# A decoder layer with 32 experts on one core: TensorE branches over an expert's third group of 32 slots where its list has at most 64 tokens

## The chip, the core and the metric

The kernel runs on one core of a Trainium2 chip. The metric is the device time of one execution in microseconds (us), the median of three runs. Engines are named as the profile names them: PE is TensorE (its weight loads apart as PEld), DVE is VectorE, ACT is ScalarE, POOL is GpSimd, and SP is SyncE, which here only issues transfers. A q behind a name is the engine's sequencer.

## What is computed

One decoder layer on 512 tokens of 1024 features, in float32: three kinds of attention, an output projection, a layer norm, and then a mixture of 32 experts of which each token takes four. The change touches the experts only. Cut to them:

```python
logits = xf @ router_w + router_b            # 512 x 32
top_v, top_e = lax.top_k(logits, 4)
gate_w = softmax(top_v)
...
def expert(e, tokens):                       # for each of 32 experts, its own tokens
    h = x[tokens] @ w_gu[e] + b_gu[e]        # 1024 -> 2048
    gate, up = h[:, 0::2], h[:, 1::2]
    gate = minimum(gate, 7); up = clip(up, -7, 7)
    return ((up + 1) * gate * sigmoid(1.702 * gate)) @ w_dn[e] + b_dn[e]   # 1024 -> 1024
...
x = layer_norm(alpha * x + sum over a token's experts of gate_w * expert)
```

512 tokens with four experts each make 2048 places, 64 an expert on average. Counted from the reference's own router on its inputs, the lists of experts 0 to 31 have 53, 68, 76, 65, 61, 70, 53, 58, 66, 59, 76, 79, 83, 69, 44, 60, 72, 70, 64, 45, 63, 66, 95, 43, 40, 73, 75, 73, 76, 44, 66 and 43 tokens. Fourteen have at most 64: experts 0, 4, 6, 7, 9, 14, 15, 18, 19, 20, 23, 24, 29 and 31. None has more than 96.

## The kernel before

The first part of the run is the attention, the router and the lists of tokens. Then `moe` goes through the experts in order. Each expert has room for `NG` = 3 groups of `SL` = 32 slots; a list that is longer than 96 would go through a loop of extra blocks at the end (line 1125 on), which is jumped over with these inputs.

Weights stay in float32 and come through a ring of 18 buffers of 1024 KB (`wring`), in the order in which they are used: per expert eight for gate_up and four for down. `ring(...).get(k)` hands out the next buffer and at once writes the transfer of the tile 18 places on, which SP can issue only when TensorE has finished with the buffer that it takes. All of these transfers stand in one queue, SP's.

For an expert, three indirect transfers on POOL gather its token rows (`gather`), TensorE transposes them (`transposed`, tile `xt`, copied out of PSUM by ACT), `gate_up` makes the bias and eight weight tiles' products for the three groups into PSUM tile `gu`, `act` does the clamped SwiGLU on DVE and ACT (`ga`), TensorE transposes that (`at`), `down` makes the second product into PSUM tile `ya`, ACT scales it by the gates, and three indirect transfers add it to the sum in memory (`accd`). The innermost loop of both products runs over four column quarters, which share the array:

```python
for g in range(NG):
    for c in range(NQ):
        nc.tensor.matmul(ps[SL * c:SL * (c + 1), g, :], lhs(g), w[:, c * 512:(c + 1) * 512], ...)
```

A float32 product is two matmuls on the chip, so the trace has 192 of them for an expert's gate_up (8 tiles, 3 groups, 4 quarters, twice) and 192 for its down. The products are pipelined over experts: TensorE does gate_up of expert e, the transposes of the next expert's rows, then down of expert e - 1, and then the transposes of `ga` of expert e. The routing for two experts at a time (`plan`) lies between.

Of the kernel before, what the change touches and what calls it, by code (L numbers as in the profile page):

```python
# [7 lines left out]
FT = mybir.dt.float32  # L8
I32 = mybir.dt.int32
# [909 lines left out]
def moe(ctx, tc, env):  # L919
# [10 lines left out]
    pst = ctx.enter_context(tc.tile_pool(name="pst", bufs=3, space=PSUM))  # L930
    nring = len(slots)

    def fetch_next(pin=False):
        if state["next"] < len(order):
            fetch(slots[state["next"] % nring], pin)
# [22 lines left out]
            nc.sync.dma_start(accd.rearrange("(s c) d -> s (c d)", c=NQ)[t * P:(t + 1) * P, :], x1all[:, t, :])  # L958

    nbi = rt.tile([P, NE + 1], I32, name="nbi")  # L960

    def count():
        cnt = rt.tile([P, NE], FT, name="cnt")
        cp = pst.tile([P, 512], FT, name="cp", tag="tr")
        for t in range(NT):
            nc.tensor.matmul(cp[:, :NE], routing.on, routing.msk[:, t, :], start=(t == 0), stop=(t == NT - 1))
        nc.vector.tensor_copy(cnt, cp[:, :NE])
        nbf = rt.tile([P, NE + 1], FT, name="nbf")
        nc.vector.tensor_scalar(nbf[:, :NE], cnt, float(CAP), None, op0=OP.is_gt)
        cge = rt.tile([P, NE], FT, name="cge")  # L970
        for b in range(2, -(-S // CAP)):
            nc.vector.tensor_scalar(cge, cnt, float(CAP * b), None, op0=OP.is_gt)
            nc.vector.tensor_add(nbf[:, :NE], nbf[:, :NE], cge)
        nc.vector.tensor_reduce(nbf[:, NE:], nbf[:, :NE], AX.X, OP.max)
        nc.vector.tensor_copy(nbi, nbf)

    bases = [1] + list(range(2, NE, 2))
    ixs, gwt = ({0: [v[:, 0, g:g + 1] for g in range(NG)]} for v in (routing.ix0, routing.gw0))
# [40 lines left out]
    def listed(xt, k, g):  # L1019

        return xt[:, 2 * g + k % 2, SL * (k // 2):SL * (k // 2 + 1)]

    def gate_up(xt, weights, pick):
        ps = psg.tile([P, NG, 512], FT, name="gu", tag="gu")

        def column_tiles(lhs, w, start, stop):
            for g in range(NG):
                for c in range(NQ):
                    nc.tensor.matmul(ps[SL * c:SL * (c + 1), g, :], lhs(g), w[:, c * 512:(c + 1) * 512], start=start,  # L1029
                                     stop=stop)  # L1030

        column_tiles(lambda g: pick.to_broadcast([G, SL]), bpart, True, False)
        for k in range(8):
            w = weights(k).rearrange("p a c -> p (a c)")
            column_tiles(lambda g: listed(xt, k, g), w, False, k == 7)
        return ps

    def act(ps):
# [8 lines left out]
        nc.vector.scalar_tensor_tensor(ga, up, 1.0, ga, op0=OP.add, op1=OP.mult)  # L1047
        return ga.rearrange("p g f -> p (g f)")

    def down(at, weights, ix, gw):  # L1050
        ya = psg.tile([P, NQ, 256], FT, name="ya", tag="ya")
        for k in range(8):
            if k % 2 == 0:
                w = weights(k // 2)
            for g in range(NG):
                for c in range(NQ):

                    nc.tensor.matmul(ya[SL * c:SL * (c + 1), g, :], listed(at, k, g), w[:, k % 2, c * 256:(c + 1) * 256],  # L1058
                                     start=(k == 0 and g % 2 == 0), stop=(k == 7), skip_group_check=True)
        y = mk.tile([P, 768], FT, name="y", tag="y", bufs=1)  # L1060
        sc = []
        for g in range(NG):
            cs = slice(g * 256, (g + 1) * 256)
            nc.scalar.activation(y[:, cs], ya[:, g, :], AF.Copy, scale=gw[g])  # L1064
            sc.append(nc.gpsimd.indirect_dma_start(out=accd, out_offset=bass.IndirectOffsetOnAxis(ap=ix[g], axis=0),  # L1065
                                                   in_=y[:, cs], in_offset=None, bounds_check=NQ * S - 1,
                                                   oob_is_err=False, compute_op=OP.add))
        for a, b in ((0, 1), (0, 2), (1, 2)):
            tc.declare_no_dep(sc[b].ins, sc[a].ins, reason="a token is in an expert's list once")
# [28 lines left out]
    start_sum(start)  # L1098
    count()
    xt = transposed(xgs.pop(1), "xt", 1)  # L1100
    for e in range(1, NE + 1):
        at = transposed(hid, "at", 2)
        if e < NE:
            if e + 2 < NE:
                begin(e + 2)
            ps = gate_up(xt, ring("gu", e), bsel[:, e:e + 1])
            if e + 1 < NE:
                xt = transposed(xgs.pop(e + 1), "xt", 1)
        down(at, ring("dn", e - 1), ixs[e - 1], gwt[e - 1])
        if e < NE:  # L1110
            hid = act(ps)

# [3 lines left out]
    g2, b2 = gb[:, 0], gb[:, 1]  # L1116


    more = ctx.enter_context(tc.tile_pool(name="more", bufs=2))
    w_gate_up, w_down = env["w_gate_up"], env["w_down"]  # L1120
    wm = [slots[-1].tile([P, 2, 1024], FT, name=f"wm{k}", tag="wring") for k in range(4)]
    why = "a count of blocks, at most ceil(S / CAP)"
# [1 line left out]
    some = nc.values_load(nbi[0:1, NE:NE + 1], min_val=0, max_val=nmax, skip_runtime_bounds_check_because=why)  # L1124
    with tc.If(some > 0):  # L1125
        with tc.For_i(0, NE) as e:
            pick = more.tile([G, 1], BF, name="pick", bufs=1)
            nc.vector.tensor_copy(pick, bsel[:, bass.ds(e, 1)])
            col = more.tile([P, NT], FT, name="col", bufs=1)
            cval = more.tile([P, NT, 5], BF, name="cval", bufs=1)  # L1130
            nc.vector.tensor_copy(col[:, None, :], routing.pos[:, bass.ds(e, 1), :])
            nc.vector.tensor_copy(cval[:, None], routing.val[:, bass.ds(e, 1), :, :])
            nb = nc.values_load(nbi[0:1, bass.ds(e, 1)], min_val=0, max_val=nmax,
# [1 line left out]
            with tc.For_i(0, nb):  # L1135
                nc.vector.tensor_scalar(col, col, -float(CAP), None, op0=OP.add)
                ip = pst.tile([P, 512], FT, name="ixp", tag="tr")
                a = mk.tile([P, NT, NG * P], BF, name="places", tag="places")
                routing.places(a, col)
                routing.listed(ip, 0, lambda t: a[:, t], cval)  # L1140
                v = more.tile([P, 1, NG, 5], FT, name="vm", bufs=1)
                nc.vector.tensor_copy(v, ip[:, :5 * NG].rearrange("p (e g v) -> p e g v", g=NG, v=5))
                ix = more.tile([P, 1, NG], I32, name="ixm", bufs=1)
                gw = more.tile([P, 1, NG], FT, name="gwm", bufs=1)
                routing.rows(msm, v, 1, ix)
                routing.gates(msm, v, 1, gw)
                ixg = [ix[:, 0, g:g + 1] for g in range(NG)]

                def stream(src, view):
                    def get(k):  # L1150
                        t = wm[k % 4]
                        nc.sync.dma_start(t, view(src, k))
                        return t
                    return get

                def gu_view(w, k):
# [66 lines left out]
```

## Time and profile before

| what | value |
|---|---|
| median of 3 runs | 1503.4 us (1502.09 to 1503.58) |
| the profiled execution, its own time | 1510.97 us |
| its span | 1509.2 us |
| mean granted clock of TensorE | 0.974 |
| TensorE busy | 1434.4 us, 95% of the span |
| share of 16 DMA engines taken by the hardware queue | 74.8% |

The profile is of one execution, some 7.6 us longer than the median of the timed runs. Busy time of an engine is the union of its instructions' spans; matmuls overlap each other, so the mean length of one is far more than what one costs. [...]

### The profile page before, as it was taken

The page shows a single profiled execution, that of the slowest core. Times are in us where ns is not written, and L with a number is a line of the kernel's source. Part 1 is how long each engine was busy: PE and PEld are TensorE (multiplying, and loading weights), DVE is VectorE, ACT ScalarE, POOL GpSimd, SP SyncE. Part 2 cuts the span into 40 slices and gives each one's busy share as a digit, 9 for nine tenths or more (in the row PEclk, how much of TensorE's full clock was granted, in tenths as well). Part 3 has the DMA queues.
Part 4 walks back from the last instruction along what each step waited for, and adds up shares of the span by engine and source line. Part 5 has one row for each costly group of instructions (what it writes and reads, how often), then busy time and mean ns, then how long its engine had stood idle before and what let it go on. Part 6 is the DMA issues. An engine that isn't in the chain of part 4 may idle for free. (4 is left out here: it accounts for less than half of the span.)

```text
span 1509.2 us, 35054 instructions
## 1 busy us (share of the span) xinstructions
PE 1434.4 (95%) x15619; PEld 725.7 (48%) x15620; DVE 413.2 (27%) x887; ACT 294.8 (20%) x683; POOL 391.7 (26%) x331
## 2 busy tenths in 40 slices
PE   8999999985999999999999999999999999999991
PEld 7777667981343444444444444444444434444450
DVE  3585565564221212112020212022020212110004
ACT  5474366530000100100000010011000001000100
POOL 5432323344021212132221212132321212121124
PEclk9999999996899999999999999999999999999996
DMA  8210216547899999999999999999999999999913
GB/s 223 66 32 2 61 40 223 184 156 272 329 358 400 373 394 378 391 380 377 384 377 393 383 400 373 388 381 381 387 382 379 383 397 375 384 375 371 369 17 117
DMA packets 126257, 454.12 MB, mean 301 GB/s; under 512 B 21416, under 2 KB 53642, under 8 KB 93334
## 3 DMA queue, kind: packets, MB, share of 16 engines
q1 hardware_dynamic: 107526, 435.00, 74.8%
q0 software_dynamic: 18432, 16.84, 5.6%
q8 instruction: 124, 2.03, 0.5%
q14 instruction: 31, 0.25, 0.0%
q10 hardware_dynamic: 144, 0.00, 0.0%
HBM read 441.26 MB, written 18.87 MB: 305 GB/s over the span
## 5 line engine op out<-in xcount | busy, mean ns | idle before, releaser
L1029 PE MATMUL gu<-wring,xt 128*32 128x512 f32 x6144 | 684.7, 595 | 1.4 <-issue 0.4
L1029 PEld LDWEIGHTS gu<-wring,xt 128*32 128x32 f32 x6144 | 211.6, 110 | 449.4 <-issue 419.3
L1065 POOL DMA_INDIRECT accd<-y,ix x96 | 151.8, 1581 | 847.9 <-ACT y L1064 828.4
L1058 PE MATMUL ya<-wring,at 128*32 128x256 f32 x6144 | 340.9, 380 | 1.4 <-ACT at L1016 1.4
L1058 PEld LDWEIGHTS ya<-wring,at 128*32 128x32 f32 x6144 | 195.8, 110 | 135.2 <-issue 7.2
L1041 DVE TENSOR_SCALAR ga<-gu 128x768 f32<-128x768 f32 x32 | 30.6, 958 | 779.0 <-PE gu L1029 779.0
L1016 ACT COPY xt<-tp 128x512 f32<-128x512 f32 x64 | 27.6, 482 | 679.5 <-PE tp L1015 614.4
L1005 POOL DMA_INDIRECT xg<-x1d,ix x96 | 100.7, 1049 | 32.3 <-issue 27.1
L1064 ACT ACTIVATE y<-ya,gw 128x256 f32<-128x256 f32 x96 | 38.5, 472 | 296.1 <-issue 219.3
L173 POOL TENSOR_TENSOR wl<-raw,wh 128x1024 fp32r<-128x1024 f32 (+2 forms) x28 | 68.1, 2439 | 93.8 <-ACT wh L170 93.8
L880 DVE TENSOR_TENSOR places<-slot,pos 128x1536 bf16<-128x1536 bf16 x31 | 54.2, 1752 | 106.8 <-PE ixp L890 106.8
L244 PE MATMUL pjt<-xh,wh 128*128 128x512 f32 (+1 forms) x136 | 52.8, 388 | 1.0 <-DVE xl L222 1.0
L244 PE MATMUL pjt<-xh,wl 128*128 128x512 f32 (+1 forms) x136 | 52.4, 385 | 0.0
L244 PE MATMUL pjt<-xl,wh 128*128 128x512 f32 (+1 forms) x136 | 52.1, 383 | 0.0
L170 ACT CAST wh<-raw 128x1024 fp32r<-128x1024 f32 (+2 forms) x28 | 29.5, 1054 | 52.9 <-issue 20.9
L1015 PEld LDWEIGHTS tp<-ident,xg 128*128 128x128 f32 x192 | 21.1, 145 | 36.8 <-issue 35.7
L1015 PE MATMUL tp<-ident,xg 128*128 128x128 f32 x192 | 30.9, 293 | 6.6 <-DMA xg<-x1d,ix 6.6
L1045 ACT ACTIVATE sg<-ga 128x768 f32<-128x768 f32 x32 | 27.4, 855 | 44.1 <-DVE ga L1041 43.7
L430 ACT ACTIVATE pr<-pr,nm 128x256 f32<-128x256 f32 (+3 forms) x64 | 33.8, 529 | 7.5 <-DVE nm L429 6.9
L1046 DVE TENSOR_TENSOR ga<-ga,sg 128x768 f32<-128x768 f32 x32 | 30.7, 958 | 12.0 <-ACT sg L1045 11.5
L1047 DVE SCALAR_TENSOR_TENSOR ga<-up,ga 128x768 f32<-128x768 f32 x32 | 30.6, 958 | 1.1
L1015 PE MATMUL tp<-ident,ga 128*128 128x128 f32 x192 | 30.6, 289 | 0.0
(323 smaller groups left out, 1313.0 us busy)
## 6 DMA issues: line engine op xcount, KB each, us to landing
wring<-in_w_gate_up_dram SPq DMA_DIRECT2D x256, 1024.0 KB
wring<-in_w_down_dram SPq DMA_DIRECT2D x128, 1024.0 KB
raw<-in_w_in_dram SPq DMA_DIRECT2D x16, 512.0 KB
raw<-in_w_out_dram SPq DMA_DIRECT2D x8, 512.0 KB
x1all<-in_x_dram SPq DMA_DIRECT2D x4, 512.0 KB
x1d<-x1all SPq DMA_DIRECT2D x4, 512.0 KB
accd<-x1all SPq DMA_DIRECT2D x4, 512.0 KB
x1all<-accd SPq DMA_DIRECT2D x4, 512.0 KB
```

The lines of the kernel that those rows point to most:

```text
L173: eng.tensor_tensor(l[:, :m], raw[:, :m], h[:, :m].bitcast(FT), op=OP.subtract)
L244: nc.tensor.matmul(ps[:, qs], a[:, k, :], b[:, k, qs], start=(k == 0 and n_ == 0), stop=(k == 7 and n_ == 2))
L430: nc.scalar.activation(pr[:, :n], pr[:, :n], AF.Exp, bias=nm, scale=-1.0, accum_out=den)
L880: ins = self.nc.vector.tensor_tensor(a, self.slot[:, None, :].to_broadcast([P, n, NG * P]), pos[:, :, None].to_broadcast([P, n, NG * P]), ...
L1005: nc.gpsimd.indirect_dma_start(out=xg[:, g * 256:(g + 1) * 256], out_offset=None, in_=x1d, in_offset=bass.IndirectOffsetOnAxis(ap=ix[g], a ...
L1015: nc.tensor.transpose(pt[:, u * P:(u + 1) * P], src[:, (a + u) * P:(a + u + 1) * P], ident)
L1029: nc.tensor.matmul(ps[SL * c:SL * (c + 1), g, :], lhs(g), w[:, c * 512:(c + 1) * 512], start=start, stop=stop)
L1041: nc.vector.tensor_scalar(ga, v[:, :, :, 0], 7.0, None, op0=OP.min)
L1046: nc.vector.tensor_mul(ga, ga, sg)
L1058: nc.tensor.matmul(ya[SL * c:SL * (c + 1), g, :], listed(at, k, g), w[:, k % 2, c * 256:(c + 1) * 256], start=(k == 0 and g % 2 == 0), sto ...
L1064: nc.scalar.activation(y[:, cs], ya[:, g, :], AF.Copy, scale=gw[g])
L1065: sc.append(nc.gpsimd.indirect_dma_start(out=accd, out_offset=bass.IndirectOffsetOnAxis(ap=ix[g], axis=0), in_=y[:, cs], in_offset=None, b ...
```

## The change

The products are split by group. Groups 0 and 1 are always made; group 2 stands in a part of its own, behind a branch that only TensorE takes on a flag of the expert (`thr`, 1 where the count is over 64). Gate_up has two such branches an expert, one after each four weight tiles, and down has one, after its four tiles. The flag is read into a register once an expert. Expert 0, which runs ahead of the loop, and the extra blocks have no branch. PSUM tiles `gu` and `ya` are made once instead of once an expert. Everything else, the gathers, transposes, `act`, the scaling and the scatters, still covers three groups. A variable `more` was renamed `extra`, which changes nothing.

```diff
+    gups = psg.tile([P, NG, 512], FT, name="gu")
+    yaps = psg.tile([P, NQ, 256], FT, name="ya")
...
+    thr = rt.tile([P, NE], I32, name="thr")
...
+        nc.vector.tensor_scalar(thr, cnt, float(2 * SL), None, op0=OP.is_gt)
...
+    def third(e):
+
+        return nc.values_load(thr[0:1, e:e + 1], engines=[mybir.EngineType.PE], min_val=0, max_val=1,
+                              skip_runtime_bounds_check_because="the result of a comparison")
+
+    def groups(more, full, part):
+
+        full()
+        if more is None:
+            part()
+        else:
+            with tc.If(more > 0):
+                part()
...
-        column_tiles(lambda g: pick.to_broadcast([G, SL]), bpart, True, False)
-        for k in range(8):
-            w = weights(k).rearrange("p a c -> p (a c)")
-            column_tiles(lambda g: listed(xt, k, g), w, False, k == 7)
+        def rows(w, k, gs):
+            if k == 0:
+                column_tiles(lambda g: pick.to_broadcast([G, SL]), bpart, True, False, gs)
+            column_tiles(lambda g: listed(xt, k, g), w, False, k == 7, gs)
+
+        for k0 in (0, 4):
+            ws = {}
+
+            def full():
+                for k in range(k0, k0 + 4):
+                    ws[k] = weights(k).rearrange("p a c -> p (a c)")
+                    rows(ws[k], k, range(2))
+
+            groups(more, full, lambda: [rows(w, k, range(2, NG)) for k, w in ws.items()])
...
+        ws = []
+
+        def full():
+            for k in range(0, 8, 2):
+                ws.append(weights(k // 2))
+                rows(ws[-1], k, range(2))
+
+        groups(more, full, lambda: [rows(w, 2 * k, range(2, NG)) for k, w in enumerate(ws)])
...
+            more[e] = third(e)
+            ps = gate_up(xt, ring("gu", e), bsel[:, e:e + 1], more[e])
...
+        down(at, ring("dn", e - 1), ixs[e - 1], gwt[e - 1], more.pop(e - 1, None))
```

The order in which the instructions stand shows what this makes of an engine's program. Names like DMAHW3_49 are the semaphores of transfers, and PE_49 is the one that TensorE raises as its matmuls end; a number behind x counts equal rows, one row here being one float32 product. On PE before, the second half of expert 2's gate_up, weight tiles 4 to 7:

```order
L1029 MATMUL gu_4531<-wring_4090,xt_4334 32x512 [waits DMAHW3_49]
L1029 MATMUL gu_4531<-wring_4090,xt_4334 32x512 x11
L1029 MATMUL gu_4531<-wring_4104,xt_4334 32x512 [waits DMAHW4_49]
L1029 MATMUL gu_4531<-wring_4104,xt_4334 32x512 x11
L1029 MATMUL gu_4531<-wring_4222,xt_4334 32x512 [waits DMAHW1_49]
L1029 MATMUL gu_4531<-wring_4222,xt_4334 32x512 x11
L1029 MATMUL gu_4531<-wring_4236,xt_4334 32x512 [waits DMAHW2_49]
L1029 MATMUL gu_4531<-wring_4236,xt_4334 32x512 x11
L1015 MATMUL tp_4657<-ident_62,xg0_3863 128x128 [waits DMASW1_49,Activation_49]
```

The same place on PE in the changed kernel. Here the row behind the compare is where the program goes on for a long list; the last unconditional branch belongs to the other path, which a short list jumps to:

```order
L1048 MATMUL gu_3862<-wring_4215,xt_4341 32x512 [waits DMAHW1_49]
L1048 MATMUL gu_3862<-wring_4215,xt_4341 32x512 x7
L1048 MATMUL gu_3862<-wring_4233,xt_4341 32x512 [waits DMAHW2_49]
L1048 MATMUL gu_3862<-wring_4233,xt_4341 32x512 x7
L1039 COMPARE_AND_BRANCH
L1048 MATMUL gu_3862<-wring_4084,xt_4341 32x512 x4
L1048 MATMUL gu_3862<-wring_4094,xt_4341 32x512 x4
L1048 MATMUL gu_3862<-wring_4215,xt_4341 32x512 x4
L1048 MATMUL gu_3862<-wring_4233,xt_4341 32x512 x4
L1039 UNCONDITIONAL_BRANCH
L1039 UNCONDITIONAL_BRANCH [waits PE_49]
L1020 MATMUL tp_4667<-ident_62,xg0_3866 128x128 [waits DMASW1_49,Activation_49]
```

Each tile's twelve products have become eight ahead of the compare and four behind it, so all four tiles are in use until the part's end. The path for a long list ends in a jump and has no wait; the path for a short list waits for PE_49, raises it for the products that were left out, and goes on.

On SP before, the transfers into the ring behind expert 1's products, with what each waits for:

```order
L85 DMA wring<-in_w_gate_up_dram 128x2048 [waits DMAHW3_49,PE_49]
L85 DMA wring<-in_w_gate_up_dram 128x2048 [waits DMAHW4_49,PE_49]
L85 DMA wring<-in_w_gate_up_dram 128x2048 [waits DMAHW5_49,PE_49]
L85 DMA wring<-in_w_gate_up_dram 128x2048 [waits DMAHW6_49,PE_49]
L85 DMA wring<-in_w_down_dram 128x2x1024 [waits DMAHW7_49,PE_49]
L85 DMA wring<-in_w_down_dram 128x2x1024 [waits DMAHW0_49,PE_49]
L85 DMA wring<-in_w_down_dram 128x2x1024 [waits DMAHW1_49,PE_49]
L85 DMA wring<-in_w_down_dram 128x2x1024 [waits DMAHW2_49,PE_49]
```

And the same transfers on SP in the changed kernel:

```order
L85 DMA wring<-in_w_gate_up_dram 128x2048 [waits DMAHW3_49,PE_49]
L85 DMA wring<-in_w_gate_up_dram 128x2048 [waits DMAHW4_49,PE_49]
L1039 UNCONDITIONAL_BRANCH
L85 DMA wring<-in_w_gate_up_dram 128x2048 [waits DMAHW5_49,PE_49]
L85 DMA wring<-in_w_gate_up_dram 128x2048 [waits DMAHW6_49,PE_49]
L85 DMA wring<-in_w_down_dram 128x2x1024 [waits DMAHW7_49]
L1039 UNCONDITIONAL_BRANCH
L85 DMA wring<-in_w_down_dram 128x2x1024 [waits DMAHW0_49,PE_49]
L85 DMA wring<-in_w_down_dram 128x2x1024 [waits DMAHW1_49,PE_49]
L85 DMA wring<-in_w_down_dram 128x2x1024 [waits DMAHW2_49,PE_49]
L1039 UNCONDITIONAL_BRANCH
```

Their order is the same, but a plain branch of SP's own stands between them wherever TensorE has one, and some transfers have lost their wait for TensorE: their buffer comes free together with that of the transfer ahead.

## Rows read from the trace of the kernel before

**Rows 1.** The page: span, busy us (share) xinstructions, DMA tenths in 40 slices.

```profile
span 1509.2 us, 35054 instructions
PE 1434.4 (95%) x15619; PEld 725.7 (48%) x15620; DVE 413.2 (27%) x887; ACT 294.8 (20%) x683; POOL 391.7 (26%) x331
...
DMA  8210216547899999999999999999999999999913
```

**Rows 2.** Stretches: us, busy PE PEld DVE ACT POOL, granted clock, DMA share, GB/s.

```profile
322.00:326.90 4.90, 2.87 (x28) 2.69 (x26) 4.44 (x12) 0.55 (x2) 2.29 (x2) 1.00 0.26 107
326.90:330.30 3.40, 3.40 (x18) 3.40 (x18) 2.55 (x12) 1.28 (x4) 0.00 (x0) 0.50 0.09 31
376.00:392.00 16.00, 15.75 (x114) 4.75 (x107) 5.79 (x8) 0.84 (x1) 0.00 (x0) 0.99 1.01 419
404.00:408.00 4.00, 4.00 (x44) 1.20 (x40) 0.00 (x0) 0.00 (x0) 0.00 (x0) 1.00 0.84 297
452.00:472.00 20.00, 20.00 (x284) 10.01 (x280) 3.74 (x4) 3.56 (x8) 2.94 (x2) 1.00 1.01 412
500.00:1380.00 880.00, 878.67 (x10712) 369.03 (x10706) 144.48 (x202) 91.01 (x205) 202.99 (x156) 1.00 1.01 383
```

**Rows 3.** Waits from 404 to 1430 us: total, times, longest.

```profile
DVE ga L1041 <- PE gu L1029: 726.9, 30, 30.6
...
PE gu L1029 <- issue: 0.4, 1, 0.4
```

**Rows 4.** The transfer queue's own waits, 404 to 1430 us: total, times, longest.

```profile
SPq L85 <- PE gu L1029: 444.6, 184, 4.9
SPq L85 <- PE ya L1058: 277.1, 115, 3.1
SPq L85 <- PE tp L1015: 84.5, 33, 3.0
```

**Rows 5.** TensorE's timeline, 466 to 546 us: start, length, line, tiles, count.

```profile
468.62 0.83 PE L1029 MATMUL gu<-bpart,bsel 96*32 96x512 bf16 x12
469.28 20.77 PE L1029 MATMUL gu<-wring,xt 128*32 128x512 f32 x192
...
490.79 10.57 PE L1058 MATMUL ya<-wring,at 128*32 128x256 f32 x192
```

**Rows 6.** TensorE's timeline, 396 to 427 us, expert 1's gate_up.

```profile
399.13 22.22 PE L1029 MATMUL gu<-wring,xt 128*32 128x512 f32 x192
```

**Rows 7.** The timeline of all engines, from 1425 us to the end.

```profile
1431.88 20.98 PE L1029 MATMUL gu<-wring,xt 128*32 128x512 f32 x192
...
1465.97 10.57 PE L1058 MATMUL ya<-wring,at 128*32 128x256 f32 x192 [1.37 <-ACT at L1016]
...
1476.66 1.21 ACT L1064 ACTIVATE y<-ya,gw 128x256 f32<-128x256 f32 x3 [10.46 <-PE ya L1058]
```

**Rows 8.** The page, DMA queues: packets, MB, share of 16 engines.

```profile
q0 software_dynamic: 18432, 16.84, 5.6%
q8 instruction: 124, 2.03, 0.5%
```

**Rows 9.** Lines 1124 and 1125: duration ns min/median/max, first and last start.

```profile
L1124 PEldq TENSOR_LOAD <-nbi x1: 484/484/484, 1475.1 to 1475.1; - x1
L1125 PEldq EVENT_SEMAPHORE  x2: 51/51/51, 1479.3 to 1479.5; - x2
L1125 DVEq COMPARE_BRANCH  x1: 72/72/72, 1456.5 to 1456.5; - x1
L1125 PEldq COMPARE_BRANCH  x1: 3602/3602/3602, 1475.7 to 1475.7; - x1
L1125 ACTq COMPARE_BRANCH  x1: 45/45/45, 1477.3 to 1477.3; - x1
```

**Rows 10.** The issue of weight transfers (line 85), 403.3 to 1430 us.

```profile
L85 SPq DMA_DIRECT2D wring<-in_w_gate_up_dram x234: 327/328/341, 403.4 to 1402.9; - x117
L85 SPq DMA_DIRECT2D wring<-in_w_down_dram x124: 367/373/423, 408.5 to 1425.0; - x124
```

More of the change, by code (lines that the diff above doesn't have):

```diff
@@ L1021, in listed, with gate_up, column_tiles @@
         return xt[:, 2 * g + k % 2, SL * (k // 2):SL * (k // 2 + 1)]
[L1023 to L1027, printed above, removed]
+    def third(e):
[8 more added lines that the diff above has]
+                part()
+    def gate_up(xt, weights, pick, more=None):
+        ps = gups
+        def column_tiles(lhs, w, start, stop, gs):
+            for g in gs:
                 for c in range(NQ):
@@ L1048, in act, with down, rows @@
         return ga.rearrange("p g f -> p (g f)")
[L1050 to L1059, printed above, removed]
+    def down(at, weights, ix, gw, more=None):
+        ya = yaps
+        def rows(w, k0, gs):
+            for k in (k0, k0 + 1):
+                for g in gs:
+                    for c in range(NQ):
+                        nc.tensor.matmul(ya[SL * c:SL * (c + 1), g, :], listed(at, k, g),
+                                         w[:, k % 2, c * 256:(c + 1) * 256], start=(k == 0 and g % 2 == 0),
+                                         stop=(k == 7), skip_group_check=True)
+        ws = []
[4 more added lines that the diff above has]
+        groups(more, full, lambda: [rows(w, 2 * k, range(2, NG)) for k, w in enumerate(ws)])
         y = mk.tile([P, 768], FT, name="y", tag="y", bufs=1)
@@ L1100, in moe @@
     xt = transposed(xgs.pop(1), "xt", 1)
+    more = {}
     for e in range(1, NE + 1):
@@ L1105, in moe @@
                 begin(e + 2)
-            ps = gate_up(xt, ring("gu", e), bsel[:, e:e + 1])
+            more[e] = third(e)
+            ps = gate_up(xt, ring("gu", e), bsel[:, e:e + 1], more[e])
             if e + 1 < NE:
                 xt = transposed(xgs.pop(e + 1), "xt", 1)
-        down(at, ring("dn", e - 1), ixs[e - 1], gwt[e - 1])
+        down(at, ring("dn", e - 1), ixs[e - 1], gwt[e - 1], more.pop(e - 1, None))
         if e < NE:
@@ L1116, in moe @@
     g2, b2 = gb[:, 0], gb[:, 1]
-    more = ctx.enter_context(tc.tile_pool(name="more", bufs=2))
+    extra = ctx.enter_context(tc.tile_pool(name="more", bufs=2))
     w_gate_up, w_down = env["w_gate_up"], env["w_down"]
@@ L1126, in moe @@
         with tc.For_i(0, NE) as e:
-            pick = more.tile([G, 1], BF, name="pick", bufs=1)
+            pick = extra.tile([G, 1], BF, name="pick", bufs=1)
             nc.vector.tensor_copy(pick, bsel[:, bass.ds(e, 1)])
-            col = more.tile([P, NT], FT, name="col", bufs=1)
-            cval = more.tile([P, NT, 5], BF, name="cval", bufs=1)
+            col = extra.tile([P, NT], FT, name="col", bufs=1)
+            cval = extra.tile([P, NT, 5], BF, name="cval", bufs=1)
             nc.vector.tensor_copy(col[:, None, :], routing.pos[:, bass.ds(e, 1), :])
@@ L1140, in moe @@
                 routing.listed(ip, 0, lambda t: a[:, t], cval)
-                v = more.tile([P, 1, NG, 5], FT, name="vm", bufs=1)
+                v = extra.tile([P, 1, NG, 5], FT, name="vm", bufs=1)
                 nc.vector.tensor_copy(v, ip[:, :5 * NG].rearrange("p (e g v) -> p e g v", g=NG, v=5))
-                ix = more.tile([P, 1, NG], I32, name="ixm", bufs=1)
-                gw = more.tile([P, 1, NG], FT, name="gwm", bufs=1)
+                ix = extra.tile([P, 1, NG], I32, name="ixm", bufs=1)
+                gw = extra.tile([P, 1, NG], FT, name="gwm", bufs=1)
                 routing.rows(msm, v, 1, ix)
```

## The prediction

> **What bounds the kernel now.** I read the page first, then the stretches, then the waits of the expert stage. The page shows TensorE busy for 95% of the span, and the DMA slices near full from slice 12 on [rows 1]. The share over the span does not say which of the two sets the pace, so I read the expert stage by itself: between 500 and 1380 us TensorE is busy 878.67 of 880 us at full clock, while the DMA share is 1.01 at 383 GB/s [rows 2]. Both look full. The waits decide it: between 404 and 1430 us TensorE waits for a weight tile in no row (its largest matmul wait is 0.4 us, on its own issue) [rows 3], whereas the transfer queue waits for TensorE to free a slot of the ring, 444.6, 277.1 and 84.5 us in three rows [rows 4]. So TensorE sets the pace; the transfers follow slot by slot.
>
> The pace: from the start of gate_up's weights for expert 1, 399.13 us [rows 6], to that for expert 31, 1431.88 us [rows 7], are 30 experts, 34.4 us each.
>
> But the transfers have little room. Weights alone ran at 419 GB/s in 376 to 392 us and at 412 GB/s in 452 to 472 us [rows 2]. An expert has 12 transfers of 1024 KB, 12.58 MB, which at 415 GB/s take 30.3 us. Gathers and scatters (the software queue) take 5.6% of the span [rows 8], 84.5 us or 2.64 us per expert. Together 32.96 us, 2.747 us per transfer slot, against TensorE's 34.4. That is 4% of room.
>
> **The change, part by part.** *What is skipped.* Gate_up's matmuls take 20.77 us, the bias 0.83, the down product 10.57 us per expert [rows 5]. A third of each is 6.92, 0.28 and 3.52, in all 10.72 us. Thirteen of the experts 1 to 31 have at most 64 tokens; expert 0 has too, but it is outside the branch. 13 x 10.72 = 139.4 us of TensorE work.
>
> *Branches that are not skipped*, 18 experts x 3 = 54. The sequencer loads the flag once an expert, compares, and jumps over two instructions at the end of the part. The only register load and compare on TensorE in this trace are those at the end: the load begins at 1475.08 us and takes 484 ns [rows 9], while the last matmuls run to 1465.97 + 10.57 = 1476.54 us [rows 7]. So the sequencer was 1.46 us ahead of the array, and a load plus a compare (45 ns on ACT, 72 on DVE [rows 9]) fit inside. I take 0.1 us each, 5.4 us; bounds 0 and 0.6 us (nothing hidden). The rows on the order show that no wait stands in this path.
>
> *Branches that are skipped*, 13 x 3 = 39. Here a wait is added: the other path raises TensorE's semaphore for the matmuls that were left out, and first waits until all earlier ones have ended. Behind it on TensorE stands the next half or the transposes. ScalarE starts 0.12 us after the last matmul's end (1476.66 against 1476.54) [rows 7]; the semaphore instruction takes 51 ns on TensorE, a near branch 45 to 72 ns [rows 9], and I add 0.2 us, an estimate, for two matmuls (20.77 us / 192 = 0.108 us each) until the array is full again. I take 0.45 us, 17.6 us in all; bounds 0.2 us and TensorE's own compare of 3602 ns [rows 9].
>
> Why I take the near price: that compare jumped over the whole loop of extra blocks, which holds a gate_up and a down product, 192 matmuls and 192 weight loads each by the rows of an expert, 768 instructions. The instruction queue brought 124 packets in 2.03 MB [rows 8], for 31239 TensorE instructions [rows 1], about 252 a packet. The far jump spans three packets; the new ones skip 64 to 128 instructions, half a packet at most. [...]
>
> *TensorE's line.* 1476.5 - 139.4 + 17.6 + 5.4 = 1360 us for its last matmul, if weights were always there: 116 us less.
>
> *The transfers' line.* They are not. A skipped expert leaves TensorE with about 25 us of work against 32.96 us of transfers, so it eats its lead in the ring (18 slots, one and a half experts) and then waits. The slots now come free in fours: a tile is held until the third group has used it, at the end of its half. The first of them after the pause comes free at 399.13 + 11.1 (half of 22.22 us [rows 6]) less three quarters of the last third, about 407.5, rather than 403.4 us, the first issue now [rows 10]; first bytes about 1.2 us after an issue (the stretch 404 to 408 has a share of 0.84, so some 0.64 of its 4 us passed before them [rows 2]). From there 234 + 124 = 358 transfers remain [rows 10], at 2.747 us 983.4 us. Experts 1 to 3 are not skipped, the ring is still full, and TensorE's pace costs the transfers about 1.5 us each, 4.5 us. After the last tile a quarter of the down product's two thirds (1.76 us) and one drain follow, 2.2 us. Sum: 407.5 + 1.2 + 983.4 + 4.5 + 2.2 = 1399 us for the last matmul, 39 us later than TensorE's own line, and 77.5 us earlier than now.
>
> *The rest.* The comparison that makes the flags is one small VectorE instruction at the 390th us, among sums that TensorE does not yet need. VectorE, ScalarE, GpSimd and SyncE each pass plain branches, three an expert at some 50 ns, off the path: VectorE waits 726.9 us for gate_up [rows 3], SyncE as said. ScalarE's and GpSimd's work for the third group is not skipped. What follows the last matmul, 32.7 us to the end of the span, stays.
>
> **Sum.** The profiled execution took 1510.97 us (span 1509.2); less 77.5 it is 1433.5. It was 7.6 us above the median of the runs, so the median goes from 1503.4 to **1426 us**.
>
> **Rivals.**
> (a) *TensorE's line holds*: the transfers go faster with a deep backlog, because the 2.64 us of the software queue overlap with the others (the share of 1.01 is more than full, so some time is counted twice). Then 1503.4 - 116 = 1387 us. For it: 419 GB/s. Against it: 412 GB/s in the stage itself.
> (b) *The transfers are already full*: the share of 1.01 at 383 GB/s is their limit, and no expert takes less than 34.4 us of transfers. Then 2.867 us each: 407.5 + 1.2 + 1026.3 + 2.2 = 1437, 39 us gained from the lead that is used up, 1464 us. Against it: SyncE's 806 us of waits for slots.
> (c) *TensorE's clock falls in the new waits.* [...] Starved in a skipped expert, TensorE has 1.73 us of work for each 2.747 us of transfer; what the clock does then no row shows. While the transfers bound, the lost time lies in their wait; if it does not, some twenty falls, each losing half of 3.4 us, cost 34 us and bring 1460 us.
> (d) *Each skip fetches instructions*: 39 x 3.6 = 140.4 us eat the 139.4, and the 5.4 of the others make it 6 us longer, 1510 us. [...]
> (e) *Every taken branch empties the sequencer*, that of the unskipped path too (it jumps over two instructions): 93 branches. From 1.5 us each the gain is gone; at 3.6 us it is 335 - 139, 1699 us. Against (d) and (e): the compares of DVE and ACT, 45 and 72 ns, which jump as well.
>
> **Chances.** Forecast 0.62, (a) 0.12, (b) 0.10, (c) 0.05, (d) 0.06, (e) 0.05. A measurement of this kernel can tell about 0.2%. Faster holds the forecast and (a) to (c), 0.89; I give 0.01 of it and of (d) to no change: faster 0.88, same 0.02, slower 0.10. The range reaches from (a), 1386, to (b) and (c), 1468.
>
> **What the profile would show.** Matmuls of gate_up and down: fewer by 13 x 128 of 12288 (6144 of each). In skipped experts TensorE idles before a half or a down product, with a weight transfer as what ended the wait, in all some 35 to 45 us, from about expert 14 on; before, hardly any. The transfer queue's waits for TensorE shrink from 806 us to some tens, at 395 to 405 GB/s in the stage. TensorE's compare rows on the new line near 0.1 us. Rows of 3 us or more there would make the forecast wrong, (d) or (e); no idle time on weights and an end at 1360 speaks for (a), a rate that stays at 383 GB/s for (b), a granted clock under 0.9 in the stage for (c).

## The result and the profile after

The changed kernel takes 1452.31 us (median of 1447.06, 1464.99, 1451.07 and 1453.55), the kernel before in the same set 1502.74 us: 0.9682 of it, 95% interval 0.9617 to 0.9747. It is faster, inside the range, and 26 us above the 1426 that was forecast. The profiled execution is the fastest of the four, 5.3 us below their median; the forecast for it was 1433.5 us, so it is 13.6 us above that. In two later sets of runs the same kernel came out at 0.9769 and 0.9786. The sets of the experiments ran on three different chips. All ratios below are to the kernel before in the same set.

The page of the profiled execution, with the number of instructions behind x, and its DMA queues (they answer to [rows 1, 8]):

```profile
span 1445.3 us, 31835 instructions
...
PE 1303.5 (90%) x13903; PEld 672.3 (47%) x13904; DVE 413.2 (29%) x888; ACT 303.0 (21%) x683; POOL 391.4 (27%) x331
...
q0 software_dynamic: 18432, 16.84, 5.6%
q8 instruction: 126, 2.06, 0.6%
```

The stretches, columns as in [rows 2]; the last two lines are the end of the transfers:

```profile
404.00:500.00 96.00, 96.00 (x1202) 39.60 (x1195) 15.39 (x20) 8.95 (x20) 15.60 (x12) 1.00 0.95 363
500.00:900.00 400.00, 375.57 (x4557) 162.33 (x4558) 74.08 (x104) 48.04 (x101) 104.69 (x81) 1.00 1.03 402
900.00:1380.00 480.00, 439.61 (x5248) 186.00 (x5244) 77.89 (x106) 58.03 (x120) 106.25 (x80) 0.98 1.02 400
...
1390.00:1400.00 10.00, 7.76 (x130) 4.58 (x130) 3.74 (x4) 1.80 (x3) 0.00 (x0) 1.00 0.73 251
1400.00:1410.00 10.00, 8.63 (x164) 4.97 (x156) 0.00 (x0) 1.20 (x3) 4.38 (x3) 1.00 0.30 54
```

TensorE's matmuls in the page's list of groups (count, then busy us, mean ns, idle before):

```profile
L1048 PE MATMUL gu<-wring,xt 128*32 128x512 f32 x5312 | 588.8, 595 | 16.9 <-DMA wring<-in_w_gate_up_dram 10.5
L1087 PE MATMUL ya<-wring,at 128*32 128x256 f32 x5312 | 312.9, 387 | 8.0 <-DMA wring<-in_w_down_dram 3.6
```

5312 each, where the work before was 6144: together 1664 fewer, 13 times 128 to the matmul. Between 500 and 1380 us the DMA rate has gone from 383 to 400 to 402 GB/s. So far this is the forecast. The waits of TensorE from 404 to 1420 us are not what was forecast (total, times, longest):

```profile
PE tp L1020 <- DVE ga L1076: 38.6, 26, 1.8
PE gu L1048 <- DMA wring<-in_w_gate_up_dram: 10.5, 14, 1.3
PE gu L1048 <- PEq L1039: 5.3, 22, 1.6
PE ya L1087 <- DMA wring<-in_w_down_dram: 3.6, 3, 1.8
```

The wait for weights is 14.1 us, not 35 to 45. Nor has the transfer queue stopped waiting for TensorE; its own waits, which answer to [rows 4], from 404 to 1430 us:

```profile
SPq L85 <- DMA wring<-in_w_gate_up_dram: 221.1, 117, 4.3
SPq L85 <- DMA wring<-in_w_down_dram: 193.2, 90, 3.7
SPq L85 <- PE gu L1048: 111.2, 42, 10.3
```

Its greatest waits are now for earlier transfers of its own, but with 83.3, 76.1 and 30.8 us in three more rows (the second of them for TensorE's sequencer) 301 us are still for TensorE, where some tens were forecast. And TensorE has a wait that no step of the prediction has: 26 times the transposes of `ga` wait for VectorE. TensorE's timeline around one of them, after expert 16's gate_up (start, length, line, tiles, count, and in brackets the idle time before and what ended it):

```profile
902.04 0.61 PE L1048 MATMUL gu<-bpart,bsel 96*32 96x512 bf16 x8 [0.21 <-DVE up L1072]
904.19 0.77 PE L1020 MATMUL tp<-ident,ga 128*128 128x128 f32 x5 [1.53 <-DVE ga L1076]
904.89 3.52 PE L1087 MATMUL ya<-wring,at 128*32 128x256 f32 x32
908.35 0.33 PE L1020 MATMUL tp<-ident,ga 128*128 128x128 f32 x1
```

The reader is to see where the transposes stand. Before, the whole down product (10.57 us [rows 5]) lay between gate_up and the transposes and covered the SwiGLU on VectorE and ScalarE. Now only its first weight tile, 32 matmuls, and a bias lie ahead of them. The order of the program shows it: for experts 1 to 3 it is as before, from expert 4 on the scheduler puts the transposes into the middle of `down`. The prediction's excerpts of the order were of experts 1 and 2. Behind the wait stands a second thing, 3.52 us for 32 matmuls that take 1.93 us elsewhere. The stretches around it show TensorE busy 3.26 of 5 us, and then its clock granted at 0.68 over the next 5:

```profile
900.00:905.00 5.00, 3.26 (x51) 1.69 (x47) 3.74 (x4) 1.85 (x4) 0.00 (x0) 0.98 1.01 423
905.00:910.00 5.00, 5.00 (x55) 2.50 (x59) 0.00 (x0) 0.81 (x2) 0.00 (x0) 0.68 1.01 415
```

The granted clock is a share of TensorE's full speed, and 0.68 is a mixture of the two levels that this trace has, 1.00 and 0.50: part of these 5 us ran at half speed. Read in stretches of 1 us, the clock in this profile falls to 0.50 behind 5 of the 26 waits, each time for 3.4 us.

Last, the end of TensorE's work:

```profile
1382.99 7.07 PE L1048 MATMUL gu<-wring,xt 128*32 128x512 f32 x64 [0.17 <-PEq L1039]
1390.39 1.93 PE L1087 MATMUL ya<-wring,at 128*32 128x256 f32 x32 [0.32 <-PEq L1039]
1394.24 0.74 PE L1020 MATMUL tp<-ident,ga 128*128 128x128 f32 x5 [1.92 <-DVEq L1166]
...
1405.52 7.11 PE L1087 MATMUL ya<-wring,at 128*32 128x256 f32 x128 [1.37 <-ACT y L1103]
```

The last matmul ends at 1405.52 + 7.11 = 1412.6 us; forecast was 1399. What follows it, 32.7 us, is as before. These 13.6 us are all that the profiled execution lies above its forecast. The start is as forecast, here the issue of weight transfers as in [rows 10]:

```profile
L85 SPq DMA_DIRECT2D wring<-in_w_gate_up_dram x234: 327/341/5570, 408.0 to 1363.3; - x117
```

So the first transfer is issued at 408.0 us, where 407.5 stood.

### The profile page after: what moved, and what is told of

It is laid out like the page before. It is cut to its first block, busy times and chain, and to the rows that moved or that the text cites. A ratio compares the mean times of both kernels' runs of the same rounds, so it can differ in the third digit from the quotient of the medians.

```text
span 1445.3 us, 31835 instructions
## 1 busy us (share of the span) xinstructions
PE 1303.5 (90%) x13903; PEld 672.3 (47%) x13904; DVE 413.2 (29%) x888; ACT 303.0 (21%) x683; POOL 391.4 (27%) x331
## 5 line engine op out<-in xcount | busy, mean ns | idle before, releaser
L1048 PE MATMUL gu<-wring,xt 128*32 128x512 f32 x5312 | 588.8, 595 | 16.9 <-DMA wring<-in_w_gate_up_dram 10.5
L1048 PEld LDWEIGHTS gu<-wring,xt 128*32 128x32 f32 x5312 | 181.3, 110 | 398.7 <-issue 351.2
L1087 PE MATMUL ya<-wring,at 128*32 128x256 f32 x5312 | 312.9, 387 | 8.0 <-DMA wring<-in_w_down_dram 3.6
L1087 PEld LDWEIGHTS ya<-wring,at 128*32 128x32 f32 x5312 | 171.1, 111 | 138.4 <-issue 35.4
L1020 PE MATMUL tp<-ident,ga 128*128 128x128 f32 x192 | 34.1, 291 | 40.5 <-DVE ga L1076 38.6
L1021 ACT COPY at<-tp 128x512 f32<-128x512 f32 x64 | 30.2, 481 | 133.2 <-PE tp L1020 133.2
L1020 PEld LDWEIGHTS tp<-ident,ga 128*128 128x128 f32 x192 | 21.9, 143 | 68.1 <-issue 68.1
L170 ACT CAST wh<-raw 128x1024 fp32r<-128x1024 f32 (+2 forms) x28 | 29.5, 1054 | 52.9 <-issue 23.5
L1048 PE MATMUL gu<-bpart,bsel 96*32 96x512 bf16 x332 | 29.7, 389 | 3.5 <-DVE up L1072 3.2
```

Source lines behind the costliest of these rows:

```text
L1020: nc.tensor.transpose(pt[:, u * P:(u + 1) * P], src[:, (a + u) * P:(a + u + 1) * P], ident)
L1021: nc.scalar.copy(dst[:, a:a + n], pt[:, :n * P].rearrange("p (u q) -> p u q", q=P))
```

## The experiments

Theory A, formed on this profile: the transfers at some 400 GB/s are the floor, as forecast, and the rest of the forecast went into the VectorE wait, what it brings with it, and the end of the stage. Rival B: the branches cost more than was put down for them. Rival C: the VectorE wait lies in the shadow of the transfers and costs nothing. Four kernels ran in each of three sets, and the kernel before with them.

**Without branches.** The 13 short experts are written into the program:

```diff
-            with tc.If(more > 0):
-                part()
+    SHORT = {4, 6, 7, 9, 14, 15, 18, 19, 20, 23, 24, 29, 31}
-            more[e] = third(e)
+            more[e] = "short" if e in SHORT else None
```

> The changed kernel with the 13 short experts written into the program: their third group is left out when the program is made, and no expert has a flag, a compare or a jump. The same matmuls are left out as at run time now. Theory A (the weight transfers at about 400 GB/s set the pace of experts 14 to 26, and the rest of the forecast went to VectorE waits of 1.5 us an expert and to falls of the clock): the branches cost little, so 1430 to 1452 us, with the transfers again at 395 to 405 GB/s between 500 and 1380 us. Rival B (the branches bound the kernel: a skip costs about 1 us or more and an unskipped branch more than 0.1 us, 39 x 1 + 54 x 0.3 = 55 us): about 1395 us, since the transfers would then leave room.

Measured 1444.64 us, 0.9561 (0.9517 to 0.9605), at 401 GB/s: theory A's figure, and far from the 1395 of rival B. Its order has some of the early transposes too (12.3 us of the VectorE wait, 9 times).

**The floor.** The same with `SHORT = set(range(1, NE))`, which leaves out the third group of the 18 long experts too.

> As the run without branches, but the third group is left out for all experts 1 to 31, also for the 18 whose lists are longer, so the tokens behind place 64 get no result from their expert. TensorE then has about 24 us of work an expert. Theory A: the transfers alone set the pace; 358 transfers at 2.74 us from about 408 us land at 1395 us or a little before, the tail gets shorter than now, 1425 to 1440 us in all. Rival B (TensorE with its branches bounds the kernel, the transfers have room): 18 x 10.7 us of work less and no branches bring it to 1300 us or below.

Measured 1432.86 us, 0.9486 (0.9444 to 0.9528). With 193 us less of TensorE work than the run above (18 x 10.72) only 12 us are gained. TensorE's waits and its last product:

```profile
PE gu L1045 <- DMA wring<-in_w_gate_up_dram: 134.8, 153, 2.6
PE tp L1020 <- DVE ga L1073: 24.5, 26, 1.5
...
1393.79 1.93 PE L1084 MATMUL ya<-wring,at 128*32 128x256 f32 x32 [1.79 <-DMA wring<-in_w_down_dram]
```

Here the weights for the very last product are what TensorE waits for, and it ends at 1395.7 us, 2 us behind them. This is the transfers' line by itself; rival B's 1300 is out.

**No expert skips.** A threshold of 0 in place of 64, so that the branches are there and nothing is skipped:

```diff
-        nc.vector.tensor_scalar(thr, cnt, float(2 * SL), None, op0=OP.is_gt)
+        nc.vector.tensor_scalar(thr, cnt, 0.0, None, op0=OP.is_gt)
```

> The changed kernel with a threshold of 0 tokens in place of 64: every expert has its flag, its compares and its jumps, none skips. It costs the 93 branches on the path that does not skip, with the held slots and the order of instructions as changed. The prediction's price: 93 x 0.1 = 9 us, 1512 us. Theory A adds the VectorE wait before the transposes, 27 x 1.5 = 40 us, in the same place: about 1550 us. Rival B (an unskipped branch costs 0.5 us or more): 1590 us or above, with TensorE's sequencer on the line of the compare as what ended the idle time.

Measured 1610.63 us, 1.0641 (1.0585 to 1.0697). That is above every theory's number for it except B's, but B's sign, the sequencer as what ends the idle time, isn't there. The rows of the waits and of the compares with the jumps at the parts' ends (duration ns min/median/max):

```profile
PE tp L1020 <- DVE ga L1076: 41.7, 27, 1.8
...
PE gu L1048 <- DVE up L1072: 5.5, 27, 0.2
...
L1039 PEldq COMPARE_BRANCH  x186: 73/126/314, 409.7 to 1578.0; - x186
```

47 us of waits for VectorE, and 98 us lost. To tell what the rest is, the wait had to go and the branches had to stay.

**The transposes put back.** In the changed kernel the transposes of `ga` are held in the order in which the program is written, behind the whole down product:

```diff
-                nc.tensor.transpose(pt[:, u * P:(u + 1) * P], src[:, (a + u) * P:(a + u + 1) * P], ident)
+                ins = nc.tensor.transpose(pt[:, u * P:(u + 1) * P], src[:, (a + u) * P:(a + u + 1) * P], ident)
+                if pin:
+                    tc.keep_in_program_order(ins)
...
-        at = transposed(hid, "at", 2)
+        at = transposed(hid, "at", 2, e > 1)
```

> The changed kernel with one thing undone: the transposes of the SwiGLU result stay behind the whole down product, as they were in the kernel before, in place of after its first weight tile. The wait of TensorE for VectorE (26 x 1.5 us) should go from the trace. Theory A: it costs what it shows where TensorE sets the pace (experts 10 to 13, 25 to 31), and nothing where the transfers do: 8 to 25 us less than the changed kernel, 1427 to 1444 us. Rival C (the transfers bound the kernel up to its end): no change, 1452 us, the wait going over into waits for weights.

Measured 1451.47 us, 0.9611 (0.9568 to 0.9654). The VectorE wait is gone, and 23.4 + 18.2 us of waits for weights stand in its place, inside the 35 to 45 of the prediction. Whether that is a gain could not be told, since the changed kernel itself wasn't in this set, and the interval of its first ratio, 0.9617 to 0.9747, overlaps with this one; it was therefore run in the next:

> The changed kernel itself, timed beside the next ones on one chip, since its ratio to the kernel before has so far been taken on other runs than the experiments. 0.968 of the kernel before by its first runs; if the chip of the first experiments is slower with the kernel before (1512 against 1503 us), 0.960 to 0.968.

Measured 1478.77 us, 0.9769 (0.9739 to 0.9800): outside what was expected. In that set ran three others.

**No branches and the transposes put back**, both edits above together.

> The 13 short experts written into the program (no branches), and the transposes behind the whole down product (no VectorE wait): both of the costs beside the transfers taken away together. Theory A (the transfers and the end of the last two experts set the time): no better than each alone, 1438 to 1447 us. Rival B (branches and the VectorE wait each hold the kernel back and add up): the two gains add up, below 1435 us.

Measured 1453.13 us, 0.9569 (0.9524 to 0.9614): no better than the run without branches alone (0.9561). The median is above the expected 1447, the ratio is in line, as the kernel before took 1515.64 us in this set. The gains don't add up, so the floor under both is the transfers (400 GB/s again).

**No expert skips, the transposes put back**, the threshold of 0 with the held transposes.

> A threshold of 0 tokens (all branches there, none skips) with the transposes behind the whole down product: the price of 93 unskipped branches alone, without the VectorE wait and what followed from it. By the prediction 0.1 us each, 9 us over the kernel before. What was left of the 103 us in the first run with threshold 0 after its waits (41.7 + 5.5) and 18 clock falls of 1.7 us is 25 us, 0.27 us each: 1530 us where the kernel before takes 1505 to 1512. If the VectorE wait was not the cause of the clock falls they stay, and it is 1560 us.

Measured 1522.55 us, 1.0038 (1.0013 to 1.0063), so 5.8 us over the kernel before, where 9 stood in the prediction and 18 to 25 in the new estimate. The waits from 404 to 1500 us have no VectorE wait before transposes, and the 820 us from 500 to 1320 show full clock:

```profile
PE gu L1050 <- DVE up L1074: 5.4, 27, 0.2
PE gu L1050 <- issue: 1.8, 5, 0.4
...
500.00:1320.00 820.00, 813.06 (x9940) 359.02 (x9936) 136.15 (x188) 86.14 (x189) 187.90 (x144) 1.00 1.00 380
```

So 93 branches that don't skip cost 6 us (2 to 10 by the interval), 0.06 us each, with the 0.2 us wait of the bias included. And the early transposes cost 6.0% here, 91 us for 41.7 us of waiting; the two kernels stand in different sets, but the gap is far beyond what the sets differ by. The groups of the two pages say where the rest went. Threshold 0 with early transposes:

```profile
L1048 PE MATMUL gu<-wring,xt 128*32 128x512 f32 x6144 | 698.2, 595 | 2.4 <-issue 1.7
...
L1087 PE MATMUL ya<-wring,at 128*32 128x256 f32 x6144 | 388.3, 401 | 3.1 <-issue 1.4
```

and with the transposes put back:

```profile
L1050 PE MATMUL gu<-wring,xt 128*32 128x512 f32 x6144 | 690.9, 596 | 2.4 <-issue 1.8
L1089 PE MATMUL ya<-wring,at 128*32 128x256 f32 x6144 | 347.0, 379 | 1.0 <-ACT at L1023 1.0
```

The same matmuls take 7.3 and 41.3 us longer, 48.6 in all; with the 41.7 of the wait that is 90.3 of the 96.4 us by which the spans of these two profiles differ (1612.2 and 1515.8 us). The down product, which follows the wait, is what got slow. Its clock is one reason: one wait of 1.81 us in the first of these kernels, the stretch with the wait and the one behind it:

```profile
606.00:610.00 4.00, 2.00 (x26) 0.74 (x16) 3.35 (x4) 1.36 (x3) 0.00 (x0) 1.00 1.03 410
610.00:614.00 4.00, 4.00 (x38) 1.96 (x39) 0.00 (x0) 0.59 (x1) 0.00 (x0) 0.62 1.05 423
...
404.00:1540.00 1136.00, 1084.74 (x12648) 476.82 (x12644) 167.37 (x230) 114.94 (x241) 228.07 (x174) 0.97 0.90 347
```

TensorE worked 2.00 of 4 us, then its clock was granted at 0.62. A mean of 0.97 over 1136 us is some 34 us of lost clock; in stretches of 1 us there are 18 falls of 3.4 us at 0.50, 31 us. With the transposes put back there is none from 420 us to the last matmul. The cutting of the product is another reason: its last 160 matmuls take 8.82 us in one piece with the transposes put back, and 1.93 + 7.11 us in two pieces where no clock falls, 0.2 us more in each of 27 experts, 6 us. That leaves some 9 to 12 us of longer matmuls that no row names.

**TensorE's own line.** The changed kernel with half of its weight transfers:

```diff
-            order += [("gu", e, k) for k in range(8)]
+            order += [("gu", e, k) for k in range(0, 8, 2)]
...
-            order += [("dn", e - 1, n) for n in range(4)]
+            order += [("dn", e - 1, n) for n in range(0, 4, 2)]
...
-            w = wt.pop((kind, e, k))
-            fetch_next()
-            return w
+            if k % 2 == 0:
+                held[0] = wt.pop((kind, e, k))
+                fetch_next()
+            return held[0]
```

> The changed kernel with half of the weight transfers: every second weight tile is not fetched, and the one before it is used twice (half of the weights are left out). The transfers then have ample room, and TensorE's own line is seen. The prediction put it at 1387 us with 0.45 us for a skip and 0.1 us for a branch that does not skip. With 1 us for a skip and 0.27 us for the others, 31 us more: 1418 us. If the transfers did not bound the changed kernel, no change: 1452 us.

Measured 1386.27 us, 0.9154 (0.9112 to 0.9195), with no wait for weights and none for VectorE (its order has the transposes behind the down product). The same edit on the kernel before:

> The kernel before with half of the weight transfers (every second weight tile is the one before it again; half of the weights are left out). The prediction said that TensorE set the pace before, so no change: within 10 us of the kernel before. Then the difference to the changed kernel with half of the transfers (0.9154 of the kernel before, about 128 us less) is the work skipped, 139.4 us, less all branches: 10 us, where the prediction put 23.

Measured 1497.74 us, 0.9920 (0.9894 to 0.9946). It is 12 us less, a little more than expected, with TensorE busy 820.00 of 820 us in 500 to 1320. So the transfers cost the kernel before some 0.8%, though it shows no wait for them. On the pages gate_up's matmuls are busy 671.1 us with half of the transfers and 684.7 us with all; what slows them no row names. Between the two, which ran in different sets, the change saves 0.0766 of 1513 us, 116 us. Of 139.4 us of skipped work 23.5 go to the branches (7 either way, by the two intervals), and less 54 x 0.06 for those that don't skip, a skip costs 0.5 us.

**Side by side.** The last set held the changed kernel and the one with the transposes put back together.

> The changed kernel once more, beside the next two on one chip. Its ratio was 0.968 and 0.977 on two sets of runs; here between these two.

> The changed kernel with the transposes behind the whole down product, this time beside the changed kernel on one chip. Theory A (the VectorE wait, and the clock falls and late instructions with it, hold TensorE behind the transfers where they are slow): 0.957 to 0.963 of the kernel before, as in its first run, 8 to 20 us less than the changed kernel. Rival C (the transfers hold the kernel anyway, and the difference between the sets was the chip): no difference to the changed kernel beyond 3 us.

Measured 1480.10 us, 0.9786 (0.9759 to 0.9813), and 1454.34 us, 0.9614 (0.9584 to 0.9645). The difference is 26 us, and the intervals are apart: in this set rival C falls, and theory A's 8 to 20 us was too little. The changed kernel's waits from 404 to 1446 us in this set:

```profile
PE tp L1020 <- DVE ga L1076: 41.2, 27, 1.8
PE gu L1048 <- PEq L1039: 11.9, 22, 3.5
PE ya L1087 <- PEq L1039: 3.0, 10, 0.3
```

and those with the transposes put back:

```profile
PE ya L1089 <- DMA wring<-in_w_down_dram: 23.3, 28, 2.3
PE gu L1050 <- DMA wring<-in_w_gate_up_dram: 18.7, 21, 1.6
...
PE tp L1020 <- PEq L1041: 4.2, 11, 0.6
PE gu L1050 <- PEq L1041: 3.7, 10, 1.0
...
PE ya L1089 <- PEq L1041: 0.8, 5, 0.2
```

The first kernel hardly waits for weights: here TensorE is the bound again. Its wait for VectorE only takes the room of the other's 42 us of waits for weights, so the idle time to the last matmul is 67.5 us in the one and 61.6 in the other. The larger part is in the busy time, 973.7 against 953.5 us. The down product alone is busy 327.1 and 308.3 us, and the mean clock of the span 0.957 and 0.965; of the 5.9 us that are idle more, the sequencer's waits, 14.9 against 8.7 us, are as much. From 420 us to the last matmul the clock falls 10 times in the first and 3 times in the second, 3.4 us at half speed each: seven falls more are some 12 of the 20 us. Eight of the 10 stand behind waits for VectorE before the transposes. The 3 stand behind waits of 2.15 to 2.24 us for a down weight tile, so in this profile the clock fell in waits for weights too.

The same program has no fixed price for its order. In its first profile that product took 312.9 us with 5 clock falls, and from the start of gate_up of expert 1 to the last matmul are 1012.9 us, as many as in the kernel with the transposes put back here (1012.8). In its two later profiles they are 1037.8 and 1038.4 us. So in the first profile the VectorE waits do lie where the other kernel waits for weights, as rival C has it, and in the other two they don't. The falls, 5 against 7 and 10, are 3 to 9 of these 25 us; the rest stays open.

**The end turned round**, with the transposes put back: for expert 31, the down product of expert 30 and its weights come ahead of gate_up.

```diff
+            if e == NE - 1:
+                down(at, ring("dn", e - 1), ixs[e - 1], gwt[e - 1], more.pop(e - 1, None))
             ps = gate_up(xt, ring("gu", e), bsel[:, e:e + 1], more[e])
```

> As the run before this, and the last two experts turned round: the down product of expert 30 and its weights come ahead of gate_up of expert 31. If the transfers end the stage (theory A), then what TensorE has left when the last weights land should shrink by a down product: from the last matmul at 1411.8 us to about 1402 us, 8 to 12 us less than the run before this. If TensorE's own work ends the stage (rival B), the order of the two products is no matter, and the SwiGLU of expert 30 stands uncovered: 3 to 5 us more.

Measured 1455.54 us, 0.9635 (0.9607 to 0.9664): no difference to the kernel with the transposes put back (0.9614) that these intervals show, where 8 to 12 us less were expected. TensorE's end:

```profile
1400.22 1.93 PE L1049 MATMUL gu<-wring,xt 128*32 128x512 f32 x16 [0.89 <-DMA wring<-in_w_gate_up_dram]
1406.27 1.51 PE L1019 MATMUL tp<-ident,ga 128*128 128x128 f32 x6 [4.12 <-DVEq L1170]
1408.03 7.84 PE L1088 MATMUL ya<-wring,at 128*32 128x256 f32 x128 [0.25 <-ACT at L1022]
```

The last gate_up tile now comes at 1400 us, and the SwiGLU of expert 31, 4.12 us, has nothing to cover it. The last matmul ends at 1415.9 us, not 1402; beside it, without the turn, at 1419.1.

## Why the prediction was right, and where it was not

*The transfers' line* was right. 2.747 us a transfer gave 1426 us, 0.9485 of the kernel before; the kernel in which only the transfers count took 0.9486 (0.9444 to 0.9528), at 402 GB/s in the stage where 395 to 405 stood. In that kernel the last product also ends as described, with 1395.7 for 1399 us. That the two ratios agree to the fourth place is luck, since its first three experts are short too. In the changed kernel itself the line holds as well: the first issue comes at 408.0 for 407.5 us; from 404 to 500 us the rate is 363 GB/s where the stage has 401, which is 38 x 96 us = 3.6 MB, 3.5 transfers or 9.6 us, where 3.5 (404 to 407.5) + 1.2 + 4.5 = 9.2 stood; and the transfers run out in the profile between 1397 and 1398 us, where 1397 stood.

*TensorE's line and the branches* were right. The difference of the two kernels with half of the transfers gives 23.5 us for all branches where 17.6 + 5.4 = 23.0 stood, and 116 us saved where 116 stood. The interval is 7 us either way, so the closeness is luck and the size is not. An unskipped branch is cheaper than thought (0.06 for 0.1 us), a skip about 0.5 for 0.45 us. Of the rivals, (a), (b) and (e) are out. Single skips have the size that (d) gives to all, though no row shows a fetch in them: "PEq L1039" ends two waits of 3.3 and 3.5 us in the last set, and the compares of the profile on record, with most near 0.2 us, have one of 2.9 us:

```profile
L1039 PEldq COMPARE_BRANCH  x147: 65/176/2886, 404.7 to 1411.2; - x147
```

The instruction queue still brings 126 packets (124 before [rows 8]), though 1664 matmuls and their loads are skipped. What the compare of 2.9 us waited for no row shows. That short jumps are spared the 3602 ns of the far one [rows 9] was the prediction's estimate, from the packets that the two span; the other 146 rows of that line, at 617 ns or less, agree with it, but no run shows why. The "some 50 ns" for the plain branches of the other engines has no row in this profile either; the nearest are the compares on line 1125 of the kernel before, 45 ns on SP and ACT, 53 on POOL and 72 on DVE.

*The step that failed in the sum* is the end: "After the last tile a quarter of the down product's two thirds (1.76 us) and one drain follow, 2.2 us". This is so only when nothing else is left. When the transfers run out, between 1397 and 1398 us, TensorE has the last 128 matmuls of one down product, a wait of 1.37 us for ScalarE and another down product ahead of it, to 1412.6 us: 15 us where 2.2 stood. It was behind, because it fell back in experts 25 to 28, four long ones in a row. Gate_up of expert 25 and of expert 29 in the first profile:

```profile
1167.20 2.22 PE L1048 MATMUL gu<-wring,xt 128*32 128x512 f32 x16 [0.20 <-DMA wring<-in_w_gate_up_dram]
...
1315.17 7.05 PE L1048 MATMUL gu<-wring,xt 128*32 128x512 f32 x64
```

That is 37.0 us each (34.5 with the transposes put back), where the prediction has 32.96 for the transfers. The prediction compared the two lines over the whole stage, but they change places along the experts, so the end isn't the later of the two. Putting the transposes back doesn't mend it: there the last matmul comes at 1411.8 and 1419.1 us in the two profiles, and the last stretch of 10 us up to it has transfers of 65 and 48 GB/s. The turned end, which was to show it, left other work uncovered, so this reading rests on the traces and not on an experiment.

The end is the 13.6 us of the profiled execution. The other 12.8 of the 26 us come from the last step of the sum: it carried over the 7.6 us by which the profile before lay above its median, and the profile after lies 5.3 us below its own.

*The other step that failed* is "Behind it on TensorE stands the next half or the transposes", with VectorE "off the path". It took the order of everything else for that of before, and of the changed order two experts were read where the rest differ. From expert 4 on the transposes stand in the middle of `down`, TensorE waits 1.5 us for VectorE in each expert, and the clock fell to 0.50 for 3.4 us behind 5 of these 26 waits in the first profile. So rival (c) was right in its mechanism: the clock fell in waits for VectorE, which it did not have, and, 3 times in the kernel with the transposes put back, in waits for weights, which it had. The 3.4 us that it counts for a fall are the stretch from 326.90 to 330.30 us of [rows 2]. Set beside its repair, the order costs 26 us. By the ratio of the result, 0.9682 against the repair's 0.9611, it is 11 us with overlapping intervals, and in the first profile it is nothing that the length of the stage shows.

Together: from the floor at 0.9486, the 18 long experts' third groups bring 0.9569; the branches 0.9614 (0.0045 between two sets and 0.0050 within one, in both cases with overlapping intervals); the order of the transposes 0.968 to 0.979. What decides between 0.968 and 0.979 from one set to the next stays open. It is not the mean clock alone: that is 0.968 over a span of 1445.3 us in the first profile and 0.967 over 1471.6 us in the second. The sets ran on different chips, and whether that is the reason no run here tells.

The version with the transposes put back is the fastest one measured here that still decides at run time: 0.961 in two sets.

## What to carry to other kernels

A branch around matmuls was cheap on TensorE here, 0.06 us unskipped and some 0.5 us skipped, but the scheduler may put the rest into another order around it, and that order has to be read for the whole program, not for the first rounds of a loop. Where TensorE was the bound, with a threshold of 0, waits of 1.5 us cost twice what their row says (91 us for 41.7), in good part through the clock (18 falls to 0.50, 31 us). Two bounds that are close to each other have to be followed round by round: which of them is behind at the end decides what is left to do there. And a single profile is one execution; a step that carries its distance to the median over to another kernel can be off by as much.

## What was not expected of the hardware

With early transposes and no skips 41.7 us of waiting cost 91 us, with the same matmuls 48.6 us longer. The kernel before loses 0.8% to its own transfers without a wait in its rows: half of the transfers left out, TensorE's busy share is 820.00 of 820 us and the time 12 us less. The prediction had TensorE's compare rows near 0.1 us. Where none skips, the 186 rows on that line are two to a branch, in turns: the compare with 73 ns (82 once), and the jump at the part's end with 169 to 186 ns (over 300 three times). The median of 126 ns lies between the two kinds.
